# Five edits to the order of transfers and splits at the seam between two stages of a hybrid decoder layer

## The chip, the cores and the metric

The kernel runs on one core of a Trainium2 chip. The metric is the device time of one execution in microseconds; the median of three runs of the kernel before is 1472.37 us (1470.88 to 1472.73).

## The reference

One layer with three head groups, for 4096 new tokens of a prompt and 64 of samples, width 1024, in float32. Everything after one input projection runs in three parts, whose outputs are joined and projected once more:

```python
z = rmsnorm(x, g_pre) @ w_in
cb, cc, ch, cg, q, k, v, ag, mq, mg = split_cols(z)
u = cc * ch
out_a = silu(cg) * cb * (conv_w[0] * u[t-2] + conv_w[1] * u[t-1] + conv_w[2] * u[t])   # causal convolution over t
out_b = silu(ag) * window_attention(q, k, v, sink)    # 8 heads, 2 key heads, window 128, blocks of 128 queries
out_c = silu(mg) * attention(mq, mem_k, mem_v)        # 4 heads, 256 memory tokens
y = concat(out_a, out_b, out_c) @ w_out
x = x + rmsnorm(y, g_post)
```

The softmax of the window has one extra term per head (the sink). The memory's keys and values are projected from memory tokens; the sample tokens use caches.

## The kernel before, in words

Float32 products are made of float32r parts: each operand is split in a high part (a cast on ACT) and a low part (a subtraction on DVE), and a product takes three matmuls: high by high, low by high, high by low. The names are hi/lo for rows (L373, L374), w for weights (L202 on ACT, L206 on DVE), mh/ml for the rows of the output projection (L1613, L1618).

**Input projection.** Tokens are taken in 8 blocks of 520, and each block needs 7 products, as in Strassen's scheme (PRODUCTS), with sums of the results on DVE (z, L390). Columns go in three phases (PHASES); the third has three column blocks, so a product of it has 36 matmuls of 128x260 (c, L383). After each column block q of a product the jobs of slots[q] are issued; this is the place at which other work is put between the products.

**Early attention.** A group is 128 queries: its window scores (ws) and memory scores (xs), softmax, the turn of the weights, and the product with the values (pv). Two groups are a chunk of 256 tokens, which has its keys (kst), queries (q) and its gate factors (mix, in which the attention's outputs are multiplied, L1359 and L1390). Groups 0, 1 and 2 begin in phase 3. third_jobs numbers its products n = 7 * (b - 1) + p, EARLY gives the n at which a group begins, and PIECES the stages with their distance from there: bands 0 and 1 in the first two products, the DVE transposes at +5 and +6, the masks (POOL, L1345) at +9 or +10. The last block's products are n = 42 to 48.

**The turn.** ACT copies the scores into the group's s buffer (L1261), DVE overwrites the masked half (L1265). After softmax, DVE transposes squares of 32x32 (turn_band L1322, turn_cross L1326), and 16 DMAs of 64 KB each (move, L1329) bring them from s to w. Only then is s free. Odd groups and groups 0 to 2 take s from one buffer (pair), the other even groups from another (sp). POOL issues the moves of groups 0 to 2, SP those of the later ones; of group 3, every second one is kept in self.moves and issued by POOL from within group 4's scores.

**Output weights.** In the last block, POOL loads them (wor, wo_load L943, 256 KB each, 16 in all), and ACT and DVE split them (wo_split), by the tables WO_LOADS and WO_SPLITS, which name the product, the slot and the weight. The tiles come from one rotating pool (wa), so that they take the places of input weights in order of use; after weight 13, gpost (the factors of the last norm) and the last two tiles are placed as well. blocks[0].split (rows mh and ml of the first output block) stands in the last product, slot 0, behind weight 13.

**Output projection.** A block is 128 tokens: 48 matmuls of 128x512 (y, L1643), in two halves of 24. events_of says what stands at which k of which half. In block i: turns of group i + 2 and i + 3, scores of group i + 3 (first half, k = 0, or later in blocks 0 and 1), values of group i + 1, loads of the next chunks, and the split of the next block's rows. After each half, DVE multiplies y by gpost (yn, L1650) and ACT squares it (L1651); tail 0 (the root, on POOL, L1664) and tail 1 (scale on ACT L1672, sum with x on POOL L1673, store by SP L1676) are issued within the next block's scores. pv shares a bank of PSUM with y's second half, so that it waits for the square. Block 1's load of chunk 3 (keys L1156, two of queries L1162) stands at the second half, k = 2, on POOL; block 2's rows are split in block 1 (high part within group 3's scores, low part near its end).

All engines run in the written order: in_order keeps it, so that an instruction that waits holds back all that stand behind it on its engine. A DMA issue by SP or POOL is an instruction of that order too.

Of the kernel before, what the change touches and what calls it, by code (L numbers as in the profile page):

```python
# [9 lines left out]
F32R = mybir.dt.float32r  # L10
# [5 lines left out]
P = 128  # L16
# [9 lines left out]
CT = 256  # L26
# [20 lines left out]
def f(ap):  # L47
    return ap.bitcast(F32)
# [3 lines left out]
def hybrid_layer(ctx: ExitStack, tc: tile.TileContext, a: dict):  # L52
# [802 lines left out]
        return jobs  # L855

    V_TURNS = range(14, 46, 4)
    EARLY = {0: 13, 1: 24, 2: 33}

    def open_group(g):  # L860
        groups[g] = Group(chunks[g // 2], g % 2)
# [5 lines left out]
              (4, 0, of("early_cross_exps")), (4, 1, of("band_weights")), (5, 0, of("early_cross_weights")), (5, 0, of("turn_band")),  # L867
              (6, 0, of("turn_cross")))
    PIECES = {0: (*STAGES, (9, 0, of("masks")), (16, 0, of("values"))), 1: (*STAGES, (9, 0, of("masks")), (15, 0, of("values"))),
              2: (*STAGES, (10, 0, of("masks")))}  # L870

    def v_load(k):
        third["v", k] = t = temp(f"vl{k}")[:, :512]
# [71 lines left out]
    def wo_split(j):  # L945
        h, k = divmod(j, KT)
        wo[k][h] = wo[k][h] or wa.tile([P, 2, 512], F32R, tag="w", name=f"wo{k}_{h}")
        w_split(wo[k][h], wo_raw.pop(j))
        if j == 13:
            gpost_place()  # L950
            wo[6][1], wo[7][1] = (wa.tile([P, 2, 512], F32R, tag="w", name=f"wo{n}_1") for n in (6, 7))

    WO_LOADS = {0: ((0, 0), (2, 1), (4, 2)), 1: ((6, 2), (8, 2)), 2: ((12, 0), (14, 0)), 3: ((10, 0),)}
    WO_SPLITS = {2: ((0, 0), (1, 1), (2, 2)), 3: ((3, 0), (4, 1), (5, 1), (6, 2)), 4: ((7, 0), (8, 1), (9, 2)),
# [20 lines left out]
    def input_projection():  # L975
        for i, (ph, b, p) in enumerate(steps):
            if ph > 0 and b == 0 and p == 0:
                h_split(i + 1)
                for fn in pending.pop(i, ()):
                    fn()  # L980
                flush()
                in_order.close()
                store_queue[0] = DMA
                own.close()
                if ph == 2:
                    kept_z.close()
                    written_order()
                open_phase(ph)
            if (ph, b, p) == (2, 0, 4):
                wb_stack.close()  # L990
                third_start()
            quads = range(len(PHASES[ph]))
            flush()
            if (ph, b, p) == (2, 1, 0):
                h_load(i + 3)
            h_load(i + (4 if ph == 2 and b else 3))
            if ph == 0 or b > 0 or p > 0:
                h_split(i + 1)
            jobs = list(pending.pop(i, ()))
            slots = third_jobs(b, p) if ph == 2 else {}  # L1000
            if ph < 2 and p < 3:
                jobs.insert(0, lambda: t_sum(ph, b, f"T{p + 2}"))
            if ph < 2:
                jobs += next_block(ph, b, p)
            if (ph, b, p) == (0, last, 2):
                jobs.append(us_load)
            if ph == 1 and NP_ * b + p + 2 in V_TURNS:
                jobs.append(lambda k=V_TURNS.index(NP_ * b + p + 2): v_load(k))
            if ph == 1 and NP_ * b + p in V_TURNS:
                jobs.append(lambda k=V_TURNS.index(NP_ * b + p): v_turn(k))  # L1010
            if (ph, b) in sums_at and p in (2, 3, 4):
                jobs.append(lambda pair=sums_at[ph, b], k=p - 2: w_sums(pair, k, sums_to[pair]))
            if (ph, b) == (1, last) and 1 <= p < 6:
                o = PRODUCTS[p - 1][0]
                for q in range(len(PHASES[2])):
                    jobs.append(lambda q=q, o=o: next_load(2, q, o))
                    pending.setdefault(i + 1, []).append(lambda q=q, o=o: next_fill(2, q, o))
            if (ph, b, p) == (1, last, 6):
                late_w = [(q, PRODUCTS[n][0]) for n in (5, 6) for q in range(len(PHASES[2]))]
                for n in range(0, 6, 2):  # L1020
                    def two(n=n):
                        t = w_slot(3, f"wn{n}")
                        for j, (q, o) in enumerate(late_w[n : n + 2]):
                            next_load(2, q, o, f(t[:, j]))
                    jobs.append(two)
                for q, o in late_w:
                    pending.setdefault(i + (3 if o == "S4" else 4), []).append(lambda q=q, o=o: next_fill(2, q, o))
            if ph == 2 and b == last:
                for j, slot in WO_SPLITS.get(p, ()):
                    slots[slot].append(lambda j=j: wo_split(j))  # L1030
                for j, slot in WO_LOADS.get(p, ()):
                    slots[slot].append(lambda j=j: wo_load(j))
                if p == 6:
                    slots[0].append(blocks[0].split)
                    slots[2].append(gpost_load)
            if (ph, b, p) in SWITCH:
                jobs = SWITCH[ph, b, p]() + jobs
            if p == 0:
                zz[b] = [[None, None] for _ in quads[::2]]
            done = 0  # L1040
            for q in quads:
                w = min(2, len(quads) - q // 2 * 2)
                if q % 2 == 0:
                    if p < 2:
                        zz[b][q // 2][1 - p] = z_tile(w, f"z{ph}_{b}_{q}_{1 - p}")
                    acc = accumulator(i, w, f"c{ph}_{b}_{q}_{p}")
                product(ws[ph, q, PRODUCTS[p][0]], hs[i], acc[:, q % 2])
                if ph == 2:
                    flush()
                if q % 2 == w - 1:  # L1050
                    evict(p, acc, *zz[b][q // 2])
                upto = len(jobs) * (q + 1) // len(quads)
                for fn in (*slots.get(q, ()), *jobs[done:upto]):
                    fn()
                done = upto
            if p == NP_ - 1:
                z_done((0, 2, 1, 3) if ph == 1 else (2, 3, 0, 1) if ph == 0 else (1, 0))
            if p >= 5:
                ends = finish(ph, b, zz[b], p - 5)
                when = {(0, 5): (1, 1, 2), (0, 6): (1, 1, 2), (2, 5): (1, 1, 1), (2, 6): (2, 3, 4)}.get((ph, p), (1,) * len(ends))  # L1060
                if b == NBLK - 1 and ph < 2:
                    when = (1,) * len(ends)
                elif ph == 1 and b == 0:
                    when = (1, *(2,) * len(ends))
                for n, fn in enumerate(ends):
                    pending.setdefault(i + when[min(n, len(when) - 1)], []).append(fn)
        nonlocal vp
        vp = ctx.enter_context(tc.tile_pool(name="vp", bufs=4, side="right"))
        for n in range(2, 4):
            half_load(n)  # L1070
        for i in sorted(pending):
            for fn in pending[i]:
                fn()
        flush()
# [63 lines left out]
    class Chunk:  # L1138
# [8 lines left out]
            return third["pre"] if self.c == 0 or self.c % 2 else bq if q else kp  # L1147

        def load_keys(self):
            c, t0 = self.c, self.t0  # L1150

            self.kst = self.pool().tile([P, 2, P + CT], F32R, tag="k", name=f"kst{c}")
            lo = P if c == 0 else 0
            if c == 0:
                G.memset(f(self.kst[:, :, 0:P]), 0.0)
            G.dma_start(self.kst[:, :, lo:], qd[:, 0, :, t0 - P + lo : t0 + CT].rearrange("a p n -> p a n"))  # L1156

        def load_queries(self, n):

            if n == 0:  # L1160
                self.q = self.pool(True).tile([P, 12, CT], F32R, tag="q", name=f"q{self.c}").rearrange("p (j a) n -> p j a n", a=2)
            G.dma_start(self.q[:, :, n], qd[n, 1:7, :, self.ts].rearrange("j p n -> p j n"))  # L1162

        def load_mix(self):

# [13 lines left out]
    class Group:  # L1179
# [32 lines left out]
        def scores(self):  # L1212
# [6 lines left out]
            tail(0)  # L1219
            if self.b == 4:  # L1220
                turn(1, 3)
                for fn in groups[3].moves:
                    fn()
                blocks[1].load()
            self.bands(bands[2:], 1)
            if self.b == 4:
# [97 lines left out]
        def turn_cross(self):  # L1324
# [4 lines left out]
            move = lambda g, k, queue: queue.dma_start(to[32 * k : 32 * k + 32, g], self.squares[32 * g : 32 * g + 32, k])  # L1329
            for g in range(4):  # L1330
                for k in range(4):
                    if b == 3 and k % 2:
                        self.moves = [*getattr(self, "moves", ()), lambda g=g, k=k: move(g, k, G)]
                    else:
                        move(g, k, G if b < 3 or b == 31 and k % 2 else DMA)
# [362 lines left out]
    def events_of(i, block):  # L1698
# [9 lines left out]
            at(0, 0, turn, 0, 3)  # L1708
        if i == 2:
            at(0, 0, turn, 0, 4)  # L1710
            at(0, 0, turn, 1, 4)
        at(0, {0: 3, 1: 4}.get(i, 0), values_and_scores, i)
        if i > 1:
# [7 lines left out]
        if i != 1:  # L1721
            at(1, 1, turn, 2, i + 2)
        if i == 1:
            at(0, 4, lambda: chunks[2].load_mix())
            at(0, 6, turn, 2, 3)
            at(1, 2, chunk_load, 3)
        if i > 0 and i + 3 < 2 * NCH:
            at(0, 5, half_load, i + 3)
        if i > 1:
            at(1, 2, turn, 0, i + 3)  # L1730
            at(1, 2, turn, 1, i + 3)
        if i:
            if i + 1 < len(blocks) and blocks[i + 1].b != 32:
                at(*((1, 3) if i < 28 else (0, 6)), blocks[i + 1].split, *((1,) if i == 1 else ()))
        for (n, p, k), stage in sample.items():
            if n == i:
                at(p, k, next, stage, None)
# [118 lines left out]
```

## Time and profile before

| | us |
|---|---|
| runs, median (lowest to highest) | 1472.37 (1470.88 to 1472.73) |
| profiled execution | 1477.29 |
| its span | 1475.6 |
| TensorE busy | 1458.6 |
| VectorE busy | 1210.2 |
| ScalarE busy | 759.5 |
| GpSimd busy | 458.2 |

The profile comes from one further execution, 4.9 us longer than the median of the runs. The granted clock of TensorE was 0.998 of full speed in the mean. The input projection ends near 939 us, and the blocks of the output projection follow, each about 16 us. PE is TensorE, DVE is VectorE, ACT is ScalarE, POOL is GpSimd, SP is SyncE; PEld is the loading of weights into TensorE, which runs beside the matmuls; SPq is the queue of SP. "[2.90 <-ACT y L1651]" behind an instruction says that its engine was idle for 2.90 us before it and that the ACT instruction of line 1651 on tile y ended that.

### The profile page before, as it was taken

The page shows a single profiled execution, that of the slowest core. Times are in us where ns is not written, and L with a number is a line of the kernel's source. Part 1 is how long each engine was busy: PE and PEld are TensorE (multiplying, and loading weights), DVE is VectorE, ACT ScalarE, POOL GpSimd, SP SyncE. Part 2 cuts the span into 40 slices and gives each one's busy share as a digit, 9 for nine tenths or more (in the row PEclk, how much of TensorE's full clock was granted, in tenths as well). Part 3 has the DMA queues.
Part 4 walks back from the last instruction along what each step waited for, and adds up shares of the span by engine and source line. Part 5 has one row for each costly group of instructions (what it writes and reads, how often), then busy time and mean ns, then how long its engine had stood idle before and what let it go on. Part 6 is the DMA issues. An engine that isn't in the chain of part 4 may idle for free.

```text
span 1475.6 us, 30886 instructions
## 1 busy us (share of the span) xinstructions
PE 1458.6 (99%) x11457; PEld 1338.8 (91%) x11457; DVE 1210.2 (82%) x1893; ACT 759.5 (51%) x1867; POOL 458.2 (31%) x636
## 2 busy tenths in 40 slices
PE   9999999999999999999999999989999999999998
PEld 9999999999999999999999999867777777777776
DVE  6879887899998877799677777988898988999853
ACT  6776655566522222244445444655655656665541
POOL 0222322312300000000002135265566556556561
PEclk9999999999999999999999999999999999999999
DMA  9989999996865644485977968998988898998773
GB/s 266 175 254 227 292 260 254 249 297 220 232 225 177 210 130 131 138 281 140 330 264 229 290 213 268 314 222 226 235 234 222 216 248 222 235 237 227 230 213 110
DMA packets 211852, 337.27 MB, mean 229 GB/s; under 512 B 55285, under 2 KB 125941, under 8 KB 211669
## 3 DMA queue, kind: packets, MB, share of 16 engines
q1 hardware_dynamic: 158517, 225.37, 52.0%
q0 software_dynamic: 44400, 79.20, 21.4%
q10 hardware_dynamic: 8784, 30.72, 6.8%
q8 instruction: 91, 1.49, 0.5%
q14 instruction: 60, 0.49, 0.1%
HBM read 192.48 MB, written 110.15 MB: 205 GB/s over the span
## 4 chain that ended last, share of the span: by engine, by line
PE 81%; DMA 8%; issue 3%; DVE 3%; SPq 2%; ACT 1%; POOL 1%; ACTq 0%; POOLq 0%; DVEq 0%
PE c L383 52%; PE y L1643 20%; PE pv L1124 5%; DMA w<-s 3%; PE ws L1124 2%; SPq L1329 2%; DMA place<-md 1%; PE mem_acc L810 1%; PE xs L1124 1%; DMA vh<-vn 1%; DMA vd<-v 0%; DMA x_1B<-in_xt 0%; DMA wr_2S<-sd4S 0%; DMA qd<-z 0%; DMA x_7T<-hd_T 0%
## 5 line engine op out<-in xcount | busy, mean ns | idle before, releaser
L1643 PE MATMUL y<-wo,mh 128*128 128x512 f32 (+1 forms) x1040 | 328.7, 391 | 0.0
L390 DVE TENSOR_TENSOR z<-c,z 128x520 f32<-128x520 f32 (+1 forms) x308 | 193.1, 643 | 69.0 <-PE c L383 67.8
L1643 PEld LDWEIGHTS y<-wo,mh 128*128 128x128 f32 x1040 | 194.2, 188 | 52.5 <-DVE wmx L1274 5.8
L1643 PE MATMUL y<-wo,ml 128*128 128x512 f32 (+1 forms) x520 | 201.1, 387 | 0.7 <-DVE ml L1618 0.7
L1314 POOL TENSOR_SCALAR s<-s,xrd 128x256 f32<-128x256 f32 x128 | 61.0, 490 | 205.1 <-DVE xrd L1311 199.5
L1643 PEld LDWEIGHTS y<-wo,ml 128*128 128x128 f32 x520 | 97.8, 188 | 19.6 <-DVE ml L1618 1.1
L1284 ACT ACTIVATE s<-s,wnm 128x128 f32<-128x128 f32 x256 | 98.7, 387 | 0.0
L756 POOL MEMSET negs<- 128x1 f32 x1 | 0.1, 99 | 285.1 <-DVE w_2A L206 285.1
L1261 ACT COPY s<-ws 128x256 f32<-128x256 f32 x128 | 41.2, 377 | 81.9 <-PE ws L1124 53.8
L1673 POOL TENSOR_TENSOR xr<-yn,xr 128x1024 f32<-128x1024 f32 x31 | 74.1, 2391 | 18.8 <-ACT yn L1672 17.4
L1345 POOL TENSOR_SCALAR_AFFINE_SELECT wd<-w 128x512 f32<-128x512 f32 x64 | 58.7, 918 | 36.7 <-DMA w<-s 19.1
L1651 ACT ACTIVATE y<-y 128x512 f32<-128x512 f32 (+1 forms) x66 | 38.5, 583 | 55.5 <-DVE yn L1650 54.8
L1265 DVE COPY_PREDICATED s<-wmask,ws 128x256 f32<-128x256 uint8 x124 | 47.8, 439 | 14.6 <-ACT s L1261 12.9
L1124 PEld LDWEIGHTS ws<-kst,q 64*128 64x128 f32 x768 | 48.0, 185 | 12.0 <-issue 9.9
L1307 ACT ACTIVATE s<-xs,xnm 128x256 f32<-128x256 f32 x128 | 58.1, 460 | 0.6 <-DVE xnm L1301 0.6
L1345 POOL TENSOR_SCALAR_AFFINE_SELECT w<-w 128x512 f32<-128x512 f32 x64 | 56.1, 897 | 2.2
L1124 PE MATMUL ws<-kst,q 64*128 64x256 f32 x768 | 55.6, 288 | 0.6 <-DVE s L1265 0.6
L1650 DVE TENSOR_TENSOR yn<-y,gpost 128x512 f32<-128x512 f32 (+1 forms) x66 | 44.6, 676 | 13.8 <-PE y L1643 12.9
L392 ACT COPY z<-c 128x520 f32<-128x520 f32 (+1 forms) x44 | 24.3, 555 | 56.7 <-PE c L383 52.4
L296 ACT ACTIVATE nat<-nat 104x1024 f32<-104x1024 f32 x40 | 42.3, 1057 | 20.8 <-DMA nat<-in_x_p 20.8
L1672 ACT ACTIVATE yn<-yn,yst 128x1024 f32<-128x1024 f32 x31 | 35.6, 1149 | 25.8 <-POOL yst L1664 25.8
L1284 ACT ACTIVATION_READ_ACCUMULATOR s<-s,wnm 128x1 f32 x256 | 47.9, 187 | 0.0
(966 smaller groups left out, 4975.9 us busy)
## 6 DMA issues: line engine op xcount, KB each, us to landing
w<-s SPq DMA_DIRECT2D x448, 64.0 KB
q<-qd POOLq DMA_DIRECT2D x32, 768.0 KB, 6.9
xr<-in_x_p SPq DMA_DIRECT2D x32, 512.0 KB
nat<-in_x_p SPq DMA_DIRECT2D x39, 416.0 KB
o_yp<-xr SPq DMA_DIRECT2D x31, 512.0 KB
md<-th POOLq DMA_DIRECT2D x48, 260.0 KB, 8.8
qd<-zh SPq DMA_DIRECT2D x48, 260.0 KB
qd<-z SPq DMA_DIRECT2D x48, 260.0 KB
```

Of the source, the lines that this page charges most:

```text
L296: S.activation(t[:RG], t[:RG], AF.Square, accum_out=r[:RG, i : i + 1])
L383: TE.matmul(bank[:, :HW], l, r, start=first and i == 0, stop=last and i == 3 * KH - 1)
L390: add = lambda dst, other: V.tensor_tensor(dst, c, other, op=ALU.add)
L1124: ins = TE.matmul(o, w, x, **kw)
L1265: V.copy_predicated(to, squares(third["wmask"]), squares(s3[:, :, 0:P]))
L1284: S.activation(sm[:, h], sm[:, h], AF.Exp, bias=nm[:, h : h + 1], scale=SCALE, accum_out=den[:, h : h + 1])
L1307: S.activation(p[:, i], s[:, i].rearrange("p (a k j) -> p a k j", a=2, k=4), AF.Exp, bias=nm[:, i : i + 1], scale=SCALE, accum_out=den[:, ...
L1314: G.tensor_scalar(p[:, i], p[:, i], rd[:, i : i + 1], 0.5, op0=ALU.mult, op1=ALU.mult)
L1345: G.affine_select(out, src, pattern=[[32 * sign, 2], [0, 8], [sign, 32]], compare_op=op, fill=0.0, base=base * sign, channel_multiplier=-s ...
L1643: TE.matmul(acc, self.hl[l][:, k], wo[k][c0 // 512][:, r, c0 % 512 : c0 % 512 + c1 - c0], start=j == 0, stop=j == passes * KT - 1)
L1650: V.tensor_tensor(yn[:m, c0:c1], acc[:m], gpost[0][:m, c0:c1], op=ALU.mult)
L1673: total = G.tensor_tensor(self.xr, yn, self.xr, op=ALU.add)
```

## The change

Five edits:

1. Group 2 begins at n = 34 instead of 33; its masks are at +9 instead of +10, so they stay at n = 43.
2. blocks[0].split moves from the last product, slot 0, to the last but one, slot 2, ahead of weight 12. Tiles wo4_1, wo5_1, gpost, wo6_1 and wo7_1 are placed before it (wo_places), in the order in which they were placed before.
3. Every second move of group 4 is kept and issued by POOL, from within group 5's scores, as was done for group 3 alone.
4. Chunk 3's keys and queries are loaded by SP and not by POOL, and in block 1's first half, k = 5, and not in its second half. Chunk 2's mix is loaded at k = 5, behind them, and not at k = 4.
5. The low part of block 2's rows is made in block 2, between the two transposes of group 4, and not near the end of block 1.

```diff
-    EARLY = {0: 13, 1: 24, 2: 33}
+    EARLY = {0: 13, 1: 24, 2: 34}
...
-              2: (*STAGES, (10, 0, of("masks")))}
+              2: (*STAGES, (9, 0, of("masks")))}
...
         w_split(wo[k][h], wo_raw.pop(j))
-        if j == 13:
-            gpost_place()
-            wo[6][1], wo[7][1] = (wa.tile([P, 2, 512], F32R, tag="w", name=f"wo{n}_1") for n in (6, 7))
+
+    def wo_places():
+        wo[4][1], wo[5][1] = (wa.tile([P, 2, 512], F32R, tag="w", name=f"wo{n}_1") for n in (4, 5))
+        gpost_place()
+        wo[6][1], wo[7][1] = (wa.tile([P, 2, 512], F32R, tag="w", name=f"wo{n}_1") for n in (6, 7))
...
             if ph == 2 and b == last:
+                if p == 5:
+                    slots[2].append(wo_places)
+                    slots[2].append(blocks[0].split)
...
                 if p == 6:
-                    slots[0].append(blocks[0].split)
                     slots[2].append(gpost_load)
...
-            c, t0 = self.c, self.t0
+            c, t0, queue = self.c, self.t0, DMA if self.c == 3 else G
...
-            G.dma_start(self.kst[:, :, lo:], qd[:, 0, :, t0 - P + lo : t0 + CT].rearrange("a p n -> p a n"))
+            queue.dma_start(f(self.kst[:, :, lo:]), f(qd[:, 0, :, t0 - P + lo : t0 + CT].rearrange("a p n -> p a n")))
...
-            G.dma_start(self.q[:, :, n], qd[n, 1:7, :, self.ts].rearrange("j p n -> p j n"))
+            (DMA if self.c == 3 else G).dma_start(f(self.q[:, :, n]), f(qd[n, 1:7, :, self.ts].rearrange("j p n -> p j n")))
...
             if self.b == 4:
                 turn(1, 3)
-                for fn in groups[3].moves:
+            if self.b in (4, 5):
+                for fn in groups[self.b - 1].moves:
                     fn()
+            if self.b == 4:
                 blocks[1].load()
...
-                    if b == 3 and k % 2:
+                    if b in (3, 4) and k % 2:
...
         if i == 2:
             at(0, 0, turn, 0, 4)
+            at(0, 0, blocks[2].split, 1)
             at(0, 0, turn, 1, 4)
...
         if i == 1:
-            at(0, 4, lambda: chunks[2].load_mix())
+            at(0, 5, chunk_load, 3)
+            at(0, 5, lambda: chunks[2].load_mix())
             at(0, 6, turn, 2, 3)
-            at(1, 2, chunk_load, 3)
...
-            if i + 1 < len(blocks) and blocks[i + 1].b != 32:
-                at(*((1, 3) if i < 28 else (0, 6)), blocks[i + 1].split, *((1,) if i == 1 else ()))
+            if 1 < i < len(blocks) - 1 and blocks[i + 1].b != 32:
+                at(*((1, 3) if i < 28 else (0, 6)), blocks[i + 1].split)
```

## The prediction, made before the kernel ran

> **What bounds the kernel now.** First the busy table of the page, then the waits of TensorE (PE) between 860 and 1000 us, which is the stretch that all five edits lie in.
>
> ```profile
> span 1475.6 us, 30886 instructions
> ...
> PE 1458.6 (99%) x11457; PEld 1338.8 (91%) x11457; DVE 1210.2 (82%) x1893; ACT 759.5 (51%) x1867; POOL 458.2 (31%) x636
> ```
> ```profile
> PE pv L1124 <- ACT y L1651: 4.3, 2, 2.9
> PE y L1643 <- DVE ml L1618: 0.7, 1, 0.7
> PE ws L1124 <- DVE s L1265: 0.6, 1, 0.6
> ```
> PE is busy for 1458.6 of 1475.6 us, so no edit gains unless it closes one of PE's few gaps. Here are all of them in this stretch (columns: what waits, for what, us in total, times, longest): 4.3 + 0.7 + 0.6 = 5.6 us in four gaps, of 1.4, 2.9, 0.7 and 0.6 us. The largest ends here (start, duration, instruction, idle time before it):
>
> ```profile
> 993.14 1.44 PE L1124 MATMUL pv<-w,mv 128*64 128x128 f32 x16 [2.90 <-ACT y L1651]
> ```
> ```profile
> 906.00:918.00 12.00, 12.00 (x103) 12.00 (x102) 7.74 (x10) 5.30 (x9) 8.42 (x15) 1.00 0.98 313
> 918.00:930.00 12.00, 12.00 (x102) 12.00 (x101) 12.00 (x19) 9.25 (x15) 4.83 (x9) 1.00 1.03 408
> ...
> 993.74:997.15 3.41, 3.41 (x26) 1.52 (x22) 1.98 (x5) 1.69 (x5) 3.03 (x5) 0.50 0.42 101
> ```
> These are the windows (length, busy time of PE, PEld, DVE, ACT, POOL, granted clock, DMA share, GB/s). After the 2.9 us gap the clock is 0.50 for 3.41 us: PE counts as busy, but does half the work, about 3.41 x 0.5 = 1.7 us lost, which no wait shows. So 5.6 + 1.7 = 7.3 us can be had at most, 0.5% of the span. The first two windows show the danger: from 906 to 930 the DMA share is about 1.0 and from 918 DVE has not a moment free.
>
> **Group 2 a product later.** Its first scores wait for ACT's copies, and those for group 1's transfers out of the shared s buffer:
>
> ```profile
> 869.60 0.37 ACT L1261 COPY s<-ws 128x256 f32<-128x256 f32 x1 [5.41 <-DMA w<-s]
> ```
> ACT stood 5.41 us and came free at 869.60; a product lasts 36 matmuls, one each 0.12 us (from 930.62 to 930.74 further down), 4.3 us, so one product later the buffer has been free for some 3.7 us. The gap of 0.6 goes: **-0.6**.
>
> What it triggers is dearer. All of group 2's stages move, so do its 16 transfers, which POOL issues; its masks stay in the same product (34 + 9 = 33 + 10), and the loads of the output weights stand behind both in POOL's order.
>
> ```profile
> 900.13 6.41 POOL L1329 DMA_DIRECT2D w<-s  x13 [5.84 <-DVE s L1326]
> ...
> 918.55 3.20 POOL L943 DMA_DIRECT2D wor<-in_w_out  x6
> ```
> ```profile
> 900.00:904.00 4.00, 0.00 (x0) 0.00 (x0) 3.87 (x8) 1.00 0.51 100
> ```
> ```profile
> DMA to landing us min/median/max: 5.1/6.4/7.7
> ```
> (The transfers' issues; a window of the w tiles alone; the landing of the 16 output-weight loads of L943.) The transfers began at 900.13, in a stretch with DMA share 0.51; 4.3 us later they begin at about 904 and push up to 0.51 x 4 = 2.0 us of DMA work into the full stretch from 906. The weights come at least 2.0 us later if every queue bears its part; at most by the 4.3 us that the transfers and masks ahead of them slip in POOL's order. Is there cover?
>
> ```profile
> 925.39 0.62 ACT L202 CAST wo<-wor 128x512 fp32r<-128x512 f32 x1 [0.73 <-DMA wor<-in_w_out]
> ```
> ```profile
> 928.70 1.23 DVE L374 TENSOR_TENSOR lo_7B<-x_7B,hi_7B 128x1040 fp32r<-128x1040 f32 x1
> ```
> ```profile
> 930.62 0.28 PE L383 MATMUL c<-lo_7B,w_0S 128*128 128x260 f32 x1
> 930.74 0.40 PE L383 MATMUL c<-hi_7B,w_0S 128*128 128x260 f32 x2
> ```
> No: the cast at 925.39 already waited 0.73 us for its load. Behind it in ACT's order stands the hi part of the next product's rows, behind that lo_7B on DVE, which ends at 928.70 + 1.23 = 929.93 for PE at 930.62: 0.7 us of slack. PE then waits 2.0 - 0.7 = 1.3 us at the lower end, and 4.3 - 0.7 = 3.6 at the upper; nothing if ACT and DVE make it up in the product before, though DVE is full. PE arrives 0.6 us earlier, which adds up to that. I take **+2.0**, bounds 0 and +4.2, nearer to the lower since the share of 0.51 was measured, the full slip is only possible. This is the largest term that is unknown.
>
> **Block 0's split a product earlier.**
>
> ```profile
> 934.99 2.25 ACT L202 CAST wo<-wor 128x512 fp32r<-128x512 f32 x4 [3.23 <-DMA wor<-in_w_out]
> ```
> ```profile
> 937.80 1.28 DVE L206 TENSOR_TENSOR wo<-wor,wo 128x512 fp32r<-128x512 f32 x2
> 939.00 1.22 DVE L1618 TENSOR_TENSOR ml<-place,mh 128x1024 fp32r<-128x1024 f32 x1
> ```
> Now ACT casts four weights (10 to 13) and then block 0's rows; afterwards the rows come behind two of them, so two casts of 0.56 us and two lo parts of weights (DVE, 0.64 each) go behind ml: it ends 1.1 to 1.3 us sooner than 939.00 + 1.22 = 940.22, against the 0.7 that is missing. The tiles are handed out in the same order, so no buffer changes. Weights 12 to 15, now later by the 1.2 us of ml, are first read half a block of y after 939 and are covered by that. **-0.7**; 0 if the load that ACT waits for at 934.99 slips by more than PE itself.
>
> **Blocks 1 to 4: three edits, one chain.** DVE, ACT, POOL and SP in turn, and the loads of queries over the whole run (KB each, median us to landing):
>
> ```profile
> 971.36 1.20 DVE L1618 TENSOR_TENSOR ml<-mix,mh 128x1024 fp32r<-128x1024 f32 x1
> 972.48 0.68 DVE L1650 TENSOR_TENSOR yn<-y,gpost 128x512 f32<-128x512 f32 x1
> 973.08 1.23 DVE L1322 STREAM_TRANSPOSE s<-s 128x1024 f32<-128x1024 f32 x1
> 974.30 1.25 DVE L1326 STREAM_TRANSPOSE s<-s 128x1024 f32<-128x1024 f32 x1
> ...
> 988.20 0.68 DVE L1650 TENSOR_TENSOR yn<-y,gpost 128x512 f32<-128x512 f32 x1
> ```
> ```profile
> 985.28 1.04 ACT L1613 CAST mh<-mix 128x1024 fp32r<-128x1024 f32 x1
> 991.84 0.65 ACT L1261 COPY s<-ws 128x256 f32<-128x256 f32 x2 [5.52 <-DMA w<-s]
> 992.38 0.60 ACT L1651 ACTIVATE y<-y 128x512 f32<-128x512 f32 x1
> ```
> ```profile
> 974.22 0.78 POOL L1156 DMA_DIRECT2D kst<-qd  x1
> ...
> 978.57 2.41 POOL L1673 TENSOR_TENSOR xr<-yn,xr 128x1024 f32<-128x1024 f32 x1 [0.59 <-ACT yn L1672]
> ```
> ```profile
> 975.62 13.18 SPq L1329 DMA_DIRECT2D w<-s  x16
> ```
> ```profile
> q<-qd POOLq DMA_DIRECT2D x32, 768.0 KB, 6.9
> ```
> (a) Block 2's split goes from 971.36 to between the two transposes. yn, its square on ACT and the pv of values 3 come 1.2 us sooner, so the 1.4 gap falls to 0.2; the second transpose waits for POOL's weights anyway and stays at about 974.4, and ml is first read a block later. But DVE runs without a pause from here to 988.88, with the same work, so at the next gap PE merely arrives 1.2 us earlier and waits longer: it counts once, with (c).
>
> (b) Group 4's transfers. SP issued 16 in 13.18 us (0.82 each) and ACT's copy of group 6 stood until 991.84, 3.0 us after the last issue. Halved: SP's eight take 6.6 us, POOL's eight 8 x 0.49 (6.41 / 13 above) = 3.9 us. Chunk 3's loads leave POOL for SP half a block earlier; POOL issued them from 974.22, just ahead of the transfers. The last transfer is issued at about 982 instead of 988.8 and lands, 3.0 later, near 985; on SP the queue holds chunk 3's loads and chunk 2's mix ahead, which is worth a us or two: 984 to 987, where ACT's need is 985.28 + 1.04 = 986.3. What is moved past: chunk 2's mix goes behind chunk 3's loads on SP, two of queries and one of keys, which is half their size; two like these take 14 us at the row's median if nothing overlaps. It is still issued in block 1's first half, before 975, and first read by the gate after pv of values 4, past 993, so that is covered. POOL's loads and its add after them come 3.9 us later, of which only the add is felt.
>
> (c) What is late next: ACT's square then waits for DVE's yn, which ends at 988.20 + 0.68 = 988.88, plus 0.76 for the square and its read (from 992.38 to pv at 993.14): pv at 989.64 instead of 993.14, -3.5. Against that: POOL's 2.41 us add (978.57) now stands behind eight issues and falls at about 982.5, when DVE divides group 5's weights. POOL's long operations hold small DVE ones:
>
> ```profile
> L1301 DVE TENSOR_SCALAR xnm<-xmx x12: 168/170/2902, 963.8 to 1050.1; 128x2 f32<-128x2 f32 x12
> ```
> The same DVE operation takes 170 ns in the median and 2902 at most. Price 0 to 2.4 (the whole add); I take 1.0, between. (a) and (c) together: **-2.5**, bounds -3.5 and -1.1. PE arrived at 993.14 - 2.90 = 990.24, now 1.2 sooner, 989.0, and waits until 990.6: 1.6 us.
>
> The half clock: a gap of 1.4 us was followed by full clock, one of 2.9 by half; 1.6 is nearer to the first, so I let the 1.7 go: **-1.7**. [...]
>
> [...]
>
> **Sum:** -0.6 + 2.0 - 0.7 - 2.5 - 1.7 = -3.5 us. The profiled execution took 1477.29; 1473.8 would be its successor. The runs' median is 1472.37, 4.9 less than the profiled one; the same difference gives **1468.9**, -0.24%. A difference under 0.2%, 2.9 us, counts as none.
>
> **Rivals.**
>
> 1. *The weights are covered and DVE isn't held* (0.18): stall 0 and -3.5 in (c): -6.5, **1465.9**. For it: ACT has time, 9.25 of 12 us busy. Against: DVE's 12.00 of 12.
>
> 2. *The clock halves again* (0.14): the 1.7 stays, -1.8: **1470.6**. For: 2.9 us sufficed; against: 1.4 did not.
>
> 3. *The transfers of group 4 land no sooner* (0.09), because the DMA engines and not SP's issues limit them: the change does not do what it says. ACT is freed at 991.84 as before, (a), (c) and the clock give nothing: -0.6 + 2.0 - 0.7 = +0.7, **1473.1**.
>
> 4. *The output weights are late by the whole product* (0.18), the slower side. Masks and transfers of group 2 slip by 4.3, the load issued at 918.55 goes at 922.9 and lands 6.4 later (median) at 929.3, where ACT wants it at 924.8: 4.5 late, 3.8 after the slack; a gap of that length is followed by half clock, +1.7, and block 0's rows are late again, so that the 0.7 stays. -0.6 + 5.5 - 2.5 - 1.7 = +0.7; with the longest landing, 7.7, +2.0; with DVE held for the whole 2.4 and the clock halved again after it, 1.4 + 1.7 more, +5.1: 1473.1 to 1477.5, **1475.3** in the middle. It makes the kernel slower from a stall of about 3.1 us on.
>
> **How the numbers follow.** Forecast 0.41, rivals 0.18, 0.14, 0.09, 0.18. Faster by over 0.2% (below 1469.4): rival 1 and 0.35 of the forecast, whose stall can be longer than 2.0: 0.53. Slower (above 1475.3): the upper half of rival 4, 0.09. Within: the rest, 0.38. Range: 1465.5 (rival 1 and a little) to 1474.0 (rival 3 and the lower edge of rival 4); outside stay some 0.14 above and 0.05 below. Alone, the forecast runs from 1466.9 (no stall) to 1471.1 (stall 4.2).
>
> **What would show it.** In the changed profile: no wait of ws on DVE's copy near 870; waits of c on a lo_7 tile between 914 and 935 (my 2.0; none for rival 1, near 4 with a half clock for rival 4); ACT's casts of wo waiting for DMA earlier than 925; no wait of y on ml; pv of values 3 without its 1.4; group 6's copies on ACT waiting for DVE or PE and not for DMA (still DMA in rival 3); the pv of values 4 with about 1.6 us and granted clock 1.00 after it (0.50 in rival 2); a DVE operation of some us while POOL adds. It is wrong above all if output weights come early or much later than supposed, or if a new gap opens past 1000 us, where I suppose nothing changes.

## The result, and the profile after

The changed kernel is slower: median 1477.75 us of 22 runs (1474.58 to 1485.71) against 1473.53 of 22 runs of the kernel before, ratio **1.0029, 95% interval 1.0017 to 1.0041**, about +4.2 us where -3.5 was forecast. The time lies outside the range of 1465.5 to 1474.0, on the side of the fourth rival, to which 0.18 was given, and just above the 1477.5 at which that rival ended.

First the head of the page of the changed kernel, and then the waits of TensorE from 860 to 1010 us, which answer to those shown of the kernel before.

```profile
span 1481.2 us, 30914 instructions
...
PE 1459.2 (99%) x11457; PEld 1338.7 (90%) x11457; DVE 1206.6 (81%) x1893; ACT 757.7 (51%) x1867; POOL 459.4 (31%) x641
```
```profile
PE c L383 <- ACT hi_7T L373: 2.9, 1, 2.9
PE ws L1128 <- ACT y L1657: 2.1, 1, 2.1
PE pv L1128 <- ACT y L1657: 1.8, 1, 1.8
PE y L1649 <- DVE s L1271: 1.0, 1, 1.0
PE c L383 <- DVE lo_7T L374: 0.9, 1, 0.9
```
Of the old gaps one is left, and it is shorter: the second pv still waits for the square (1.8, was 2.9). In place of the others stand two waits of c in the last block's products (2.9 and 0.9), which the kernel before does not have, and two in blocks 1 and 2 (ws 2.1, y 1.0). The sum is 8.7 us, where it was 5.6.

**The products.** From the timeline ACT's first cast of an output weight, in the kernel before and in the changed one, then PE's two matmuls that waited, then the window from 918 to 940 us (columns as before, the granted clock third from the end):

```profile
918.66 1.14 ACT L202 CAST wo<-wor 128x512 fp32r<-128x512 f32 x2
```
```profile
925.45 0.62 ACT L202 CAST wo<-wor 128x512 fp32r<-128x512 f32 x1 [5.87 <-DMA wor<-in_w_out]
```
```profile
930.05 0.39 PE L383 MATMUL c<-hi_7T,w_0S 128*128 128x260 f32 x1 [2.92 <-ACT hi_7T L373]
931.33 0.58 PE L383 MATMUL c<-lo_7T,w_0S 128*128 128x260 f32 x1 [0.89 <-DVE lo_7T L374]
```
```profile
918.00:940.00 22.00, 18.20 (x126) 17.79 (x126) 16.11 (x26) 10.60 (x16) 9.70 (x17) 0.84 0.89 304
```
ACT stood 5.87 us for the first weight, where the kernel before did not wait for it at all. The next rows' cast came behind, and PE stood for 2.92 + 0.89 us. The window shows the granted clock at 0.84 in the mean of 22 us: 0.16 x 22 = 3.5 us more, so that these products cost some 2.9 + 0.9 + 3.5 = 7.3 us; from their first matmul to the first of y they took 7.1 us longer. Why the weight was late stands in POOL's timeline, of the kernel before and then of the changed one, and in the landing times of the changed kernel's 16 loads:

```profile
907.40 1.48 POOL L1329 DMA_DIRECT2D w<-s  x3 [0.86 <-DMA w<-s]
910.74 1.11 POOL L943 DMA_DIRECT2D wor<-in_w_out  x2 [1.86 <-PE c L383]
912.19 1.07 POOL L943 DMA_DIRECT2D wor<-in_w_out  x2 [0.34 <-PE c L383]
913.64 1.07 POOL L943 DMA_DIRECT2D wor<-in_w_out  x2 [0.38 <-PE c L383]
914.71 2.41 POOL L1345 TENSOR_SCALAR_AFFINE_SELECT wd<-w 128x512 f32<-128x512 f32 x2
```
```profile
905.27 6.40 POOL L1335 DMA_DIRECT2D w<-s  x13 [3.94 <-DVE s L1332]
913.28 0.50 POOL L1335 DMA_DIRECT2D w<-s  x1 [1.60 <-DMA w<-s]
913.95 0.50 POOL L1335 DMA_DIRECT2D w<-s  x1 [0.17 <-issue]
915.31 0.50 POOL L1335 DMA_DIRECT2D w<-s  x1 [0.87 <-DMA w<-s]
916.36 2.69 POOL L943 DMA_DIRECT2D wor<-in_w_out  x5 [0.55 <-DMA w<-s]
919.81 0.54 POOL L943 DMA_DIRECT2D wor<-in_w_out  x1 [0.76 <-DMA w<-s]
923.71 1.51 POOL L1351 TENSOR_SCALAR_AFFINE_SELECT wd<-w 128x512 f32<-128x512 f32 x2 [3.36 <-DMA w<-s]
```
```profile
DMA to landing us min/median/max: 3.9/4.7/10.4
```
In the kernel before, the first six loads stand between the last transfer and the masks, and POOL had waited 1.86 us for PE before the first of them, at 910.74. In the changed kernel the last of group 2's transfers wait at issue for earlier ones to land (1.60 and 0.87), so do the weights' loads (0.55, 0.76), and the masks wait 3.36 for the last transfer. The first weight was issued at 916.36, 5.6 us later, where PE's products were only 0.8 us later. The slowest of the 16 loads took 10.4 us to land, against 7.7 in the profile before; but this differs from execution to execution (10.3 and 7.5 in two more of the kernel before, 7.8 and 9.8 in two more of the changed one), so that it is the late issue that the change brought.

**Blocks 1 and 2.** The timelines of POOL, then of DVE:

```profile
983.86 4.01 POOL L1335 DMA_DIRECT2D w<-s  x8
991.47 0.76 POOL L1160 DMA_DIRECT2D kst<-qd  x1 [3.60 <-DMA w<-s]
992.25 2.39 POOL L1679 TENSOR_TENSOR xr<-yn,xr 128x1024 f32<-128x1024 f32 x1
```
```profile
994.66 0.69 DVE L1656 TENSOR_TENSOR yn<-y,gpost 128x512 f32<-128x512 f32 x1 [3.73 <-POOL xr L1679]
```
The eight transfers are issued by 987.87, but chunk 4's key load behind them waits 3.60 us until a transfer has landed, and the add stands behind the key load. Until it has read the old yn, DVE may not write the new one: DVE stands 3.73 us, the square is late, and PE waits for it, first with ws, then with pv.

### The profile page after: what moved, and what is told of

It reads as the page before. It is cut to its first block, busy times and chain, and to the rows that moved or that the text cites. A ratio compares the mean times of both kernels' runs of the same rounds, so it can differ in the third digit from the quotient of the medians.

```text
span 1481.2 us, 30914 instructions
## 1 busy us (share of the span) xinstructions
PE 1459.2 (99%) x11457; PEld 1338.7 (90%) x11457; DVE 1206.6 (81%) x1893; ACT 757.7 (51%) x1867; POOL 459.4 (31%) x641
## 4 chain that ended last, share of the span: by engine, by line
PE 78%; DMA 9%; issue 4%; DVE 4%; ACT 2%; POOL 2%; SPq 1%; ACTq 0%; POOLq 0%; DVEq 0%
PE c L383 47%; PE y L1649 21%; PE pv L1128 5%; PE ws L1128 3%; DMA w<-s 1%; DMA nat<-in_x_p 1%; DMA place<-in_xt 1%; PE xs L1128 1%; DMA wr_3A<-in_w_in 1%; PE mem_acc L810 1%; DMA wor<-in_w_out 1%; DMA md<-th 1%; DMA place<-md 1%; DMA wr_3S<-sd6S 1%; DMA vd<-v 1%
```

## The experiments

The kernels of a group ran on one chip and share the runs of the kernel before. Each row: ratio to the kernel before with its 95% interval, and what PE waited for between 860 and 1010 us in the profiled execution.

| kernel | ratio | PE's waits there, us |
|---|---|---|
| e1, group 2 back | 1.0009 (0.9996 to 1.0022) | ws 2.2, pv 1.1, y 0.9, xs 0.2 |
| e2, group 2's edit alone | 1.0024 (1.0010 to 1.0038) | c 2.1 and 0.9, pv 2.2 and 0.9, y 0.4 |
| e3, group 2's transfers by two queues | 1.0023 (1.0004 to 1.0041) | ws 2.2, c 1.6 and 0.2, y 1.1, pv 0.6, ws 0.3 |
| e4, group 1 earlier | 1.0015 (1.0001 to 1.0029) | pv 2.4 in three, ws 1.8, y 0.5 |
| e5, add first | 1.0002 (0.9991 to 1.0014) | pv 2.6 in two, y 0.8, ws 0.6 |
| e6, group 4's transfers by SP | 1.0010 (1.0000 to 1.0020) | pv 2.9 and 0.3, y 0.5 and 0.3, xs 0.4 |
| e7, float32 loads | 1.0008 (0.9997 to 1.0019) | pv 3.0 and 0.7, y 0.2 |
| e8, the two splits alone | 1.0004 (0.9995 to 1.0013) | pv 2.4, y 0.9 |

One more figure of every profile separates them: how long the last five products took, from their first matmul to the first of y. With group 2 at n = 33 it is 21.6 to 21.9 us (the kernel before in three profiles, e1 and e4 to e8), with group 2 at 34 it is 25.6 to 28.7 (the changed kernel in three profiles, e2 26.7, e3 25.6).

### e1: group 2 back

```diff
-    EARLY = {0: 13, 1: 24, 2: 34}
+    EARLY = {0: 13, 1: 24, 2: 33}
-              2: (*STAGES, (9, 0, of("masks")))}
+              2: (*STAGES, (10, 0, of("masks")))}
```

> The changed kernel with group 2 at product 33 again (masks at +10), the other four edits kept. Theory A (the loss is edit 1 alone: group 2's transfers stand a product later ahead of the output weights): the 2.9 and 0.9 us waits of c and the half clock after them go, and what is left are the gains of the other edits, about 1.0 at the first y and 1.2 in blocks 1 to 3: 2.2 us faster than before, ratio 0.9985. Rival B (the loss comes from the other edits or from the loads' new form, and the waits in the last block only take the place of others): as slow as the changed kernel, ratio 1.002 to 1.004.

The waits of c are gone, as theory A has it, and the ratio falls by 0.0020, 2.9 us (against another group of runs). But no gain against the kernel before appeared: the other four edits together are worth nothing that 12 runs show. And the wait of ws on group 1's transfers, 0.6 in the kernel before, **did not come back**, though group 2 stands where it stood. So theory A is right on where the loss is and wrong on what is left.

### e2: group 2's edit alone

```diff
-    EARLY = {0: 13, 1: 24, 2: 33}
+    EARLY = {0: 13, 1: 24, 2: 34}
-              2: (*STAGES, (10, 0, of("masks")))}
+              2: (*STAGES, (9, 0, of("masks")))}
```

> The kernel before with edit 1 alone (group 2 at product 34, masks at +9). Theory A: 1.0 us gained at group 2's first scores, 7.0 lost in products 4 to 6 of the last block, so 5 to 6 us slower than before, ratio 1.0035 to 1.004, with a wait of c on hi_7T near 3 us. Rival B: 0.6 to 1 us faster, ratio 0.9995.

The loss comes with this edit alone, 3.5 us by the ratio, less than the 5 to 6 expected. The wait of c is there (2.1 and 0.9).

### e3: group 2's transfers by two queues

```diff
-                        move(g, k, G if b < 3 or b == 31 and k % 2 else DMA)
+                        move(g, k, G if b < 2 or b == 2 and k % 2 == 0 or b == 31 and k % 2 else DMA)
```

> The changed kernel, but group 2's sixteen transfers are issued by POOL (even) and SP (odd) instead of POOL alone; group 2 stays at product 34. It tells two forms of theory A apart. A1 (order on POOL: the weights' loads are issued late since POOL stands in the transfers' issues, 913 to 916): the first load is issued some 4 us sooner, the waits of c go, and the time is 3 us under before, ratio 0.998. A2 (the DMA engines: about 2 us of transfer work moved into a full stretch, whoever issues it): the first weights still land some 4 us or more after ACT asks, c waits 1.5 to 3 us, ratio 1.000 to 1.002.

POOL issues the first weight at 911.91. The timelines of ACT, with the first casts, and of DVE:

```profile
919.82 1.14 ACT L202 CAST wo<-wor 128x512 fp32r<-128x512 f32 x2
```
```profile
922.54 1.04 DVE L390 TENSOR_TENSOR z<-c,z 128x520 f32<-128x520 f32 x2 [4.42 <-DMA qd<-z]
923.49 0.69 DVE L426 TENSOR_TENSOR z<-z,zh 128x520 fp32r<-128x520 f32 x1
924.10 1.24 DVE L374 TENSOR_TENSOR lo_7T<-x_7T,hi_7T 128x1040 fp32r<-128x1040 f32 x1
```
The first casts wait for no load any more: that wait was POOL's order (A1). But now DVE stands 4.42 us for a store of the projection (qd<-z) that must leave its tile first, and lo_7T is late behind it; c still waits 1.6 us for it, and the time did not improve. This looks like the same backlog of transfers at another victim (A2), with a DMA share of 1.03 from 918 to 930 us. It is not shown: SP issues these stores, and in this run it stood in its eight transfers until 910.47, so that its first store behind them went at 910.58, where the changed kernel's went at 907.15. Whether the stores were late by SP's order or by the full DMA engines, the run does not separate.

### e4: group 1 earlier

On top of e1:

```diff
-    EARLY = {0: 13, 1: 24, 2: 33}
+    EARLY = {0: 13, 1: 23, 2: 33}
-             1: (*STAGES, (9, 0, of("masks")), (15, 0, of("values"))),
+             1: (*STAGES, (10, 0, of("masks")), (16, 0, of("values"))),
```

> As e1, with group 1 a product earlier as well (product 23; its masks and values stay where they are): group 1's transfers then leave the s buffer a product before group 2 asks for it, so that the 0.6 us gap of group 2's scores goes without moving group 2's transfers. Theory A: 0.7 to 1.0 us faster than e1, about 3 under before, ratio 0.998. If s is not what group 2 waits for, no gain over e1; if group 1 itself waits for group 0 or for chunk 0's loads at product 23, slower than e1 by that wait.

No gain, against the 0.7 to 1.0 us expected: in e1 there was no wait of ws on that buffer left to be taken away. The interval lies just above 1; why pv waits in three places here was not tried.

### e5: the add ahead of the key load

On top of e1:

```diff
-            for fn in loads[:1]:
+            for fn in loads[: self.b != 5]:
                 fn()
             tail(1)
-            for fn in loads[1:]:
+            for fn in loads[self.b != 5 :]:
                 fn()
```

> The changed kernel with group 2 at product 33, and with chunk 4's key load put behind POOL's add (tail 1) in group 5's scores instead of ahead of it. Theory S (in blocks 1 to 3 the new bound is POOL's order: eight of group 4's transfers and the key load, which waits 3.7 us until an earlier transfer has landed, hold the add of the row sums until 982, and DVE's yn, which writes what that add reads, waits 3.8 us for it): the add begins near 978, yn's wait goes, the wait of ws on the square (2.2) goes and that of pv falls below 0.5, with no half clock: 3.5 to 5 us faster than the kernel with group 2 back alone, ratio to before 0.997. Rival (yn waits for DVE's or PE's work anyway): below 1 us, ratio 1.000 to 1.001.

The timelines of POOL, then of DVE:

```profile
973.18 4.01 POOL L1335 DMA_DIRECT2D w<-s  x8
977.20 2.40 POOL L1679 TENSOR_TENSOR xr<-yn,xr 128x1024 f32<-128x1024 f32 x1
980.43 0.76 POOL L1160 DMA_DIRECT2D kst<-qd  x1 [0.83 <-DMA w<-s]
```
```profile
976.46 3.18 DVE L1307 TENSOR_SCALAR xnm<-xmx 128x2 f32<-128x2 f32 x1
```
The add runs straight behind the transfers, and DVE's yn no longer waits for POOL; the wait of ws falls from 2.2 to 0.6. So theory S is right about who held whom. What comes next ends nearly as late: a DVE operation that takes 0.17 us elsewhere lasts 3.18, until the add has ended, and pv waits 2.2 us, where below 0.5 was expected. Most of the expected gain is not there: the profiled execution is the shortest of its twelve (span 1468.4), but the ratio to the kernel before is 1.0002 against e1's 1.0009, some 1 us better and not 3.5 to 5. The version ties with the kernel before; none of these kernels beats it clearly.

### e6: group 4's transfers by SP

On top of e1, edit 3 undone:

```diff
-                    if b in (3, 4) and k % 2:
+                    if b == 3 and k % 2:
```

> The changed kernel with group 2 at product 33 and all sixteen transfers of group 4 on SP again (edit 3 undone, chunk 3's loads still early on SP). Theory S: POOL's add comes at its old place and yn does not wait for it; instead ACT's copies of group 6 wait for the transfers as before, some 4 to 6 us, and pv waits 2 to 3 us: the time is about that of before, ratio 0.999 to 1.001. Rival (the early loads of chunk 3 alone free the transfers): group 6's copies wait under 2 us and the kernel is 3 us faster than before, 0.998.

ACT's waits from 960 to 1000 us:

```profile
ACT s L1265 <- DMA w<-s: 3.1, 1, 3.1
```
Group 6's copies again wait for the transfers, 3.1 us where the kernel before had 5.5 (4.6 and 4.4 in two more profiles), and pv 2.9; DVE's yn does not wait for POOL's add. So theory S is right, though the copies' wait is under the 4 to 6 us expected: chunk 3's early loads alone free the buffer a microsecond or two sooner at most, and not in time.

### e7: loads on float32 views

```diff
-            G.dma_start(self.kst[:, :, lo:], qd[:, 0, :, t0 - P + lo : t0 + CT].rearrange("a p n -> p a n"))
+            G.dma_start(f(self.kst[:, :, lo:]), f(qd[:, 0, :, t0 - P + lo : t0 + CT].rearrange("a p n -> p a n")))
-            G.dma_start(self.q[:, :, n], qd[n, 1:7, :, self.ts].rearrange("j p n -> p j n"))
+            G.dma_start(f(self.q[:, :, n]), f(qd[n, 1:7, :, self.ts].rearrange("j p n -> p j n")))
```

> The kernel before with the one part of the change that no edit names: the loads of keys and queries are issued on float32 views of both sides, not on float32r ones. Theory: it halves POOL's packets (44,000 to about 23,000 in the changed kernel's profile) and takes 3% off the DMA engines' time, none of which is on PE's path: ratio 1.000 within 0.001. Rival: the larger packets hold other queues up, so that it is slower by 1 us or more, ratio 1.001.

Packets fall (below), and the interval holds 1. It cannot tell a loss of a microsecond from none.

### e8: the two splits alone

Edits 2 and 5 of the change on the kernel before, with the diff shown there.

> The kernel before with edits 2 and 5 alone (block 0's rows split a product earlier; block 2's low part in block 2). Theory: the wait of the first y on ml (0.7) goes and the pv of values 3 waits 1.2 us less, which comes back at the next pv, whose 2.9 us wait grows to about 4 since it ends with group 4's transfers: 0.9 us faster than before, ratio 0.9995, within the noise; the waits show it. Rival: both count, 2.1 us, ratio 0.9985.

The first y waits for nothing and the pv of values 3 for nothing; instead y behind it waits 0.9 for DVE, and the next pv 2.4, which did not grow to the 4 expected. The two edits only moved the wait (3.3 us in all, where two more profiles of the kernel before have 3.5 and 3.8), and no gain shows.

### e9 to e12: the same kernels profiled again

e1, e7 and e8 left group 2 where it was, and none had the 0.6 us wait of ws. So both kernels were profiled twice more, unchanged.

> The kernel before, unchanged, profiled once more. Theory D (the profiled execution, 4.9 us over the median of its runs, was long because its waits were: the gaps differ from execution to execution with the moments at which transfers land, so that edits cut to close them close what most executions don't have): the 0.6 us wait of ws on group 1's transfers is absent, as in two runs that left group 2 alone (float32 loads; splits alone), the waits of y and of pv of values 3 are shorter than 0.7 and 1.4, the span is 3 to 5 us shorter. Rival (a profile adds about 4.9 us everywhere and the gaps are the same each time): the same four gaps to 0.2 us, and the profiled time near 1477 again.

> The kernel before, unchanged, a third profile, for the same question: theory D expects another set of waits, within 2 us in sum of the second one; the rival the same four gaps.

The waits of the kernel before, second execution (1474.42 us), then third (1473.21 us):

```profile
PE pv L1124 <- DMA vh<-vn: 2.8, 1, 2.8
PE pv L1124 <- ACT y L1651: 0.7, 1, 0.7
```
```profile
PE pv L1124 <- DMA vh<-vn: 1.9, 1, 1.9
PE pv L1124 <- ACT y L1651: 1.5, 1, 1.5
PE y L1643 <- DVE ml L1618: 0.2, 1, 0.2
PE ws L1124 <- DVE s L1265: 0.2, 1, 0.2
```
Theory D holds in the main: 3.5 and 3.8 us in all instead of 5.6, y's wait on ml 0 and 0.2 instead of 0.7, that of ws 0 and 0.2 instead of 0.6. The pv of values 3 waits 0.7 and 1.5, the second no less than the 1.4 of the first profile. The pv of values 4 waits 2.8 and 1.9; the view names a load of values (vh), but ACT's read of the square ends 0.05 us before this pv in all three profiles, so that it may be the square as before. The rival, a constant 4.9 us that the profile adds, is wrong: these two profiled executions lie within 1 us of the median of 22 runs, 1473.53.

> The changed kernel, unchanged, profiled once more. Theory D: the first profile, 5.2 us over its median, showed an unusually long stall in the products; here ACT's first cast of a weight still waits some us for its load (before: none), but c waits 1 to 3 us in all instead of 3.8, and the span is near 1476. Rival: c waits 3.8 us and the half clock follows, as in the first.

> The changed kernel, unchanged, a third profile, for the same question: theory D expects waits of c that differ by over 0.5 us from the first and the second; yn's wait for POOL's add in block 2 (3 to 4 us) is in all three, since it follows from the order on POOL.

In the changed kernel c waits 1.7 + 0.9 us in the second and 1.6 + 0.9 in the third profile (1478.71 and 1475.54 us), where the first had 2.9 + 0.9: theory D again, though the two agree with each other, against what was expected of the third. ACT's first cast waits 4.1 and 3.5 us for its load, and yn's wait for the add is 3.3 and 3.5: both always there. How long the last five products take, from the timeline of PE in the third profile of each kernel, the kernel before first (their first matmul, and the first one of y):

```profile
915.98 0.29 PE L383 MATMUL c<-hi_7T,w_0S 128*128 128x260 f32 x1
...
937.62 0.39 PE L1643 MATMUL y<-wo,mh 128*128 128x512 f32 x1
```
```profile
914.26 0.29 PE L383 MATMUL c<-hi_7T,w_0S 128*128 128x260 f32 x1
...
940.43 0.40 PE L1649 MATMUL y<-wo,mh 128*128 128x512 f32 x1
```
21.64 us before and 26.17 after: **+4.5 us**, of which 2.5 are c's waits and the rest is the half clock behind them (0.73 in the window from 925 to 930: 0.27 x 5 = 1.4; 0.96 in the ten after it, 0.4). In the first profiles it was 21.65 and 28.72, in the second 21.65 and 26.10.

## Why the prediction was wrong, point by point

**The bound** was right: PE at 99%, and only its gaps count, with the half clock behind a long one (0.50 behind the 2.9 us in the kernel before).

**The sum of what can be had, 7.3 us, was too large.** It was read from one execution that was 4.9 us over the median; the text took the 4.9 as a difference that stays. Two more profiles show waits of 3.5 and 3.8 us. The 0.6 of ws and the 0.7 of y, taken as terms, are about 0.1 each in the mean of the other two, so the gains of edits 1 and 2 were the closing of gaps that most executions hardly have. The two gaps of pv stay, 3.4 us in both, and so does the half clock behind them (0.89 from 985 to 1000 us in each of the three).

**Group 2, +2.0 for the weights:** the path was right (POOL's order, the load, ACT's cast, the next rows' parts, c). It measured +4.5 in the second and third profile and +7.1 in the first. The stall itself, 2.5 us and 3.8 in the first profile, lies within the bounds of 0 and 4.2. The step that failed is the half clock behind it, which the forecast put at nothing here and gave to the fourth rival alone; it came after a stall of 1.6 + 0.9 us, little longer than the one that was forecast, and makes up most of the rest. That rival came nearest: a stall of 3.8 us with the half clock behind it is what the first profile shows. The place was off too: not all of the loads stand behind the masks, as the text says. The first six stand ahead of them, and those were hit: ACT waited 5.9, 4.1 and 3.5 us for the first weight, a product before the cast at 925 that was taken for the weakest. Counted from the first of the five products, that weight was issued 4.8, 4.2 and 4.1 us later than before, about the 4.3 that the text put as its bound and thought only possible.

**Block 0's split, -0.7:** right in mechanism, in no profile of a kernel with this edit does y wait for ml; worth 0 to 0.2 in the usual execution.

**(a) Block 2's split:** pv of values 3 came sooner as said, but y behind it then waits 0.5 to 1.1 for DVE, in every profile of a kernel with this edit. In e1 DVE's second transpose waits 0.83 for POOL, as said, and the copies of group 5 come behind; that these would hold y was not seen.

**(b) Group 4's transfers:** right in what it was for: in no profile of the changed kernel does a copy of group 6 wait for them. But the 3.0 us to land that the text took was short: POOL's eight took 7.1, 6.6 and 6.7 us in the median.

**(c) What is late next, -2.5:** the step failed. 4.3 - 2.5 = 1.8 us of waits were to be left in blocks 1 to 3, and 4.5 to 4.9 are. The add was priced by the DVE operations that it slows, and not by who waits for it to have read its inputs: yn could not be written until the add was done. Nor was the 3.6 us wait of the key load in between seen. e5 shows that the other price is real too: with the first gone, a small DVE operation lasts 3.0 us longer (3.18 less 0.17), where 2.4 was the bound.

**The half clock, -1.7:** in blocks 1 to 3 it is gone in the first and third profile of the changed kernel (1.00 from 970 to 1000 us) and there in the second; e1 has it after waits of 2.2 and 1.1 (0.86 from 970 to 995 us). In the products it came new. Nearly the same waits had it and had it not: 1.9 and 1.8 us, some 4 us apart, left the clock full in the third profile (1.00 from 992 to 1000 us), and 1.7 and 1.8 us at the same place left 0.79 in the same window of the second. So the length of a gap does not decide alone, and a choice by the nearer length, as in the forecast, is luck. What else decides, the traces do not show.

**The sum in what was measured:** take the three profiles of each kernel in the mean. Up to the last five products they took 916.6 us before and 915.9 after, these products 21.65 and 27.0, and from the first y to the end 535.0 and 534.5. The loss of 4.1 us is thus in the products, +5.4, and the ratio's 2.5 to 6.0 us hold it; the other two differences, -0.7 and -0.5, are smaller than what the profiles of one kernel differ by. In blocks 1 to 3 waits of 4.5 to 4.9 stand against 4.3, 3.4 and 3.4 with the half clock's 1.7 in the kernel before, which the changed kernel has in one profile of three: nothing sure was won there. Against the forecast, some 3.4 us were lost in the products beyond the +2.0, some 4 us of the -4.2 of (a), (c) and the half clock were not won, nor some 1.1 of the -1.3 of edits 1 and 2. One more microsecond lies where no edit is: between 1378 and 1387 us pv waits 0.9 to 1.0 us for the square in the changed kernel, in all three profiles, and in none of the kernel before. There two DMA issues of ACT stand ahead of the copies and wait for DVE's ml. Why DVE is later there was not tried; every profile of a kernel with edits 2 and 5 has this wait, e5 alone excepted, and e2 and e7, without them, do not.

## What to carry to other kernels

Profile the kernel two or three times before counting a gap as a gain: here four gaps of 0.6 to 2.9 us fell from 5.6 us to 3.5 and 3.8 in other executions of the same program, and for both kernels the profile that lay farthest above the median had the longest waits of its three. An edit that closes a small gap by moving a stage moves all that the stage issues: look where they land and what stands behind them in the order of the engine that issues them. Here the DMA engines were nearly full there (a share of 0.91 from 918 to 930 us in the changed kernel, 1.03 in e3), and when two queues shared the issues, another engine was late (DVE, by 4.42 us in e3). When work is put ahead of an instruction, ask not only what that instruction slows, but what waits for it to have read its inputs.

## What the runs showed of the hardware

An operation of DVE on two numbers per partition, 0.17 us in the median, lasted 3.18 us in e5: it began 0.74 us before POOL's add of 128x1024 (2.40 us) and ended 0.04 us after the add's end. What held it before the add began is not shown. In the kernel before, three larger operations of DVE (0.41, 0.68 and 0.68 us) ran beside the add, and this one, which began 0.77 us before the add's end, lasted 0.80, until that end. Another one there, at 963.80, lasted 2.90: it began 0.45 us before POOL's add at 964.25 (2.41 us) and ended 0.04 us after the add's end.

The loads of float32r data by POOL take fewer packets when issued on float32 views. The queues of the kernel before, then of e7, same bytes:

```profile
q0 software_dynamic: 44400, 79.20, 21.4%
```
```profile
q0 software_dynamic: 23376, 79.20, 18.6%
```
The share of the DMA engines' time falls by 2.8 points. No time is gained by it here.

A DMA issue on POOL can itself wait for transfers issued well before it: 3.60 us for the key load behind eight transfers, 0.83 in e5. Whether the chip or a semaphore of the program holds it, the traces do not show.
